# Running sums of a state-space scan as rows from memory, and joined small products, beside streamed weight products

## The chip, the cores and the metric

One core of one Trainium2 chip runs the whole program. The metric is the time of one execution in microseconds (us), the median of the runs shown; lower is better. The engines are TensorE (PE), VectorE (DVE), ScalarE (ACT), GpSimd (POOL) and SyncE (SP), which here issues nearly all DMA transfers.

## What is computed

A backbone of two layers over 256 context tokens and 256 latent tokens of width 1024. Each layer modulates and normalises its tokens, feeds them to three mixers in parallel (a scan in both directions, a windowed attention, a convolution module), merges these by gates, and then has a feed-forward part (dense in layer 0, two of eight experts in layer 1). Layer 1 mixes the context only as far as the latents need it. The change lies in the scan and in attention:

```
def ssd_scan(xs, dt, a, bm, cm, h0):
    cs = jnp.cumsum(dt.reshape(nb, nc, q, n_groups, hg) * a.reshape(n_groups, hg), axis=2)
    cs_t = jnp.moveaxis(cs, 2, -1)
    decay = jnp.exp(jnp.where(lower, cs_t[..., :, None] - cs_t[..., None, :], -jnp.inf))
    scores = jnp.einsum('bclgn,bcsgn->bcgls', cm, bm)
    y_diag = jnp.einsum('bcgls,bcgels,bcsgep->bclgep', scores, decay, xd)
    decay_end = jnp.exp(cs[:, :, -1:] - cs)
    states = jnp.einsum('bcsgn,bcsge,bcsgep->bcgepn', bm, decay_end, xd)
    ...
    y_off = jnp.einsum('bclgn,bcgepn,bclge->bclgep', cm, h_in, jnp.exp(cs))
    y = (y_diag + y_off).reshape(nb, seq_len, n_heads, hp)

def na_context(q, k, v):
    s = jnp.einsum('bihd,bjhd->bhij', q, k, preferred_element_type=jnp.float32) * NA_HEAD_DIM ** -0.5
    p = jax.nn.softmax(s, axis=-1).astype(v.dtype)
    o = jnp.einsum('bhij,bjhd->bihd', p, v)
```

The scan has 16 heads of 64 in 2 groups, chunks of 128 tokens (four in layer 0's two streams, two of them latent) and two directions. Attention has 8 heads of 64.

## The kernel before

**Weight products.** Every product with a weight is three fp32r products (high by high, high by low, low by high halves; L204 to L206 in `wstat`, L250 to L252 in `wmov`). A weight tile of 128x1024 comes by one DMA on SP into one of three raw buffers (`raw`, L120); ACT makes its high half (L115), DVE its low half (L116). Tiles on PE are 128x512 with 512 tokens moving in layer 0, 256 in layer 1.

**Background.** `mix(l)` (L560) walks a list of steps, for layer 0 `glu dt qkv xbc ssd g1 p1 g2 p2 z g0 p0`. The weight products of these steps are the foreground. Beside them run generators: `conformer` (a convolution of 31 taps on DVE, L558, then a layer norm whose sums are the products `lnm`, L797), `attention` (L702) and `ssd` (L907). Each `yield` gives a price; `pump` lets a generator go on at a rate per weight product (`RATE`: conv 2.0, att 3.6, ssd 3.8 in layer 0). What a generator would do on PE it puts off: `defer(q, f, depth)` runs the function two steps later, so that its operands are ready when its place in PE's order comes, and `issue_after` the last weight product places it there. Attention must be done before `p1` (products named wb0na_out in layer 0), the conformer before `p2` (wb0conf_out), the scan before `p0` (wb0ssd_out); `g0` to `g2` are the gates (wg). A scheduler fixes each engine's order from these priorities before the run. Small products share four PSUM banks (`pw`); weight products have four more.

**Attention** (L702 to L776). For each pair of heads, a step makes the scores (S, L735), the exponentials, and then per head and query block puts off one `turned`: the transposes of the probabilities (L725) and the copy out of PSUM (L727, DVE for one head and ACT for the other). `values` puts off the products with v (po, L771), 64 columns wide.

**Scan.** `dt_path` (L839) makes the running sums `cs`. `states` (L917) puts off, per direction, one state product (st, L932). `ssd_y` (L994) makes, for each chunk, group, direction and four heads: four transposes that spread the running sum of a head over the partitions (cb, L1023), four differences with a floor on ACT (L1026), an exponential (L1027), the product with the scores (L1028), and puts off `diag`: four products (yd, L1035), each with 64 stationary columns. `off` puts off, per direction, four transposes (pe, L1050) of the exponentials, which ACT spread (rep, L1044), with four products (yo, L1051), a copy by ACT (E, L1054) and the sums on DVE.

Of the kernel before, what the change touches and what calls it, by code (L numbers as in the profile page):

```python
# [9 lines left out]
F32 = mybir.dt.float32  # L10
F32R = mybir.dt.float32r
I32 = mybir.dt.int32
AF = mybir.ActivationFunctionType
# [12 lines left out]
G = 2  # L26
# [27 lines left out]
class Body:  # L54
    def __init__(self, ctx, tc, a, out, dbg=None, stop=None):
        self.ctx, self.tc, self.a, self.out = ctx, tc, a, out
        self.dbg, self.stop = dbg, stop
        self.nc = tc.nc
        self.bg = []
        self.last = None  # L60
        ep = ctx.enter_context
        self.cst = ep(tc.tile_pool(name="cst", bufs=1))

# [638 lines left out]
    def attention(self, l, q, kT, v, nt, o_):  # L702
# [4 lines left out]
        q_ = []  # L707
        for q0, nk, lat in streams:
            nkb = nk // 128
            for hp in range(4):  # L710
# [5 lines left out]
                def turn(P, j, qb, PT=PT, nm=nm, nk=nk, nkb=nkb, st=st):  # L716

                    nc.vector.tensor_scalar(P, P, st[:, j, qb, 5:6], None, op0=ALU.mult)

                    def turned():  # L720
                        if not PT:
                            PT.update({i: self.t4(f"PT{nm}{i}").rearrange("p (k t) -> p k t", t=256) for i in range(2)})
                        pt = self.pw(f"PT{nm}{j}{qb}")
                        for kb in range(nkb):
                            nc.tensor.transpose(pt[:, kb * 128:(kb + 1) * 128], P[:, kb * 128:(kb + 1) * 128], self.con("id"))  # L725
                        ev = nc.scalar.copy if j else nc.vector.tensor_copy
                        ev(PT[j][:, :nkb, qb * 128:(qb + 1) * 128], pt[:, :nk].rearrange("p (k t) -> p k t", t=128))  # L727
                    self.defer(q_, turned)
                if lat:
                    for qb in range(2):  # L730
# [17 lines left out]
                        for j in range(2):  # L748
                            turn(P[j], j, qb)
                            yield 1.7  # L750
                else:
# [6 lines left out]
                    for j in range(2):  # L758
# [5 lines left out]
                        for qb in range(2):  # L764
                            turn(P[j][:, qb * 256:(qb + 1) * 256], j, qb)
                        yield 1.5
# [7 lines left out]
                self.defer(q_, values)  # L774
                yield 0.5
        yield from self.undefer(q_)  # L776

# [121 lines left out]

    def xs_t(self, b, half, name):  # L900
# [6 lines left out]
    def ssd(self, l, nt):  # L907
# [9 lines left out]
        def states(b, dirs, use):  # L917
# [6 lines left out]
            for g in range(G):  # L924
                px = self.xs_t(b, g, "s" + nm)
                for r in dirs:
# [67 lines left out]
    def ssd_y(self, nm, b, hin, q_):  # L994
# [5 lines left out]
        ecs = self.wk.tile([128, 2, H], F32, name=f"ecs{nm}{b}", tag="ecs", bufs=2)  # L1000
        nc.scalar.activation(ecs, cs[:, b], AF.Exp)
# [9 lines left out]
        for g in range(G):  # L1011
# [5 lines left out]
            st = {}  # L1017
            for r in range(2):
                for hq in range(2):
                    h0 = g * 8 + hq * 4  # L1020
                    pb = self.pw(f"cb{nm}{b}{g}{r}{hq}")
                    for i in range(4):
                        nc.tensor.transpose(pb[:, i * 128:(i + 1) * 128], cs[:, b, r, h0 + i:h0 + i + 1].to_broadcast([128, 128]), self.con("id"))  # L1023
                    M = self.t2(f"M{nm}{b}{g}{r}{hq}").rearrange("p (h l) -> p h l", h=4)
                    for i in range(4):
                        nc.scalar.activation(M[:, i, :], pb[:, i * 128:(i + 1) * 128], AF.Relu, bias=cs[:, b, r, h0 + i:h0 + i + 1], scale=-1.0)  # L1026
                    nc.scalar.activation(M, M, AF.Exp, scale=-1.0)  # L1027
                    nc.vector.tensor_tensor(M, M, scm[:, r, g, None, :].to_broadcast([128, 4, 128]), op=ALU.mult)  # L1028

                    def diag(r=r, hq=hq, M=M, g=g, xd=xd, st=st):  # L1030
                        if "pd" not in st:
                            st["pd"] = self.pw(f"yd{nm}{b}{g}")
                        for i in range(4):
                            hl = hq * 4 + i
                            nc.tensor.matmul(st["pd"][64 * (i % 2):64 * (i % 2) + 64, (hl // 2) * 128:(hl // 2 + 1) * 128],  # L1035
                                             xd[r][:, hl * 64:(hl + 1) * 64], M[:, i, :],
                                             start=(r == 0 and hl < 2), stop=(r == 1 and hl > 5), skip_group_check=True)
                    self.defer(q_, diag)
                    yield 1.8
            for r in range(2):  # L1040
                if hin[r] is None:
                    continue
                rep = self.t2(f"rep{nm}{b}{g}{r}")
                nc.scalar.activation(hd(rep), ecs[:, r, g * 8:(g + 1) * 8, None].to_broadcast([128, 8, 64]), AF.Copy)  # L1044

                def off(r=r, g=g, rep=rep, st=st):
                    pe = self.pw(f"pe{nm}{b}{g}{r}")
                    po = self.pw(f"yo{nm}{b}{g}{r}")
                    for i in range(4):
                        nc.tensor.transpose(pe[:, i * 128:(i + 1) * 128], rep[:, i * 128:(i + 1) * 128], self.con("id"))  # L1050
                        nc.tensor.matmul(po[:, i * 128:(i + 1) * 128], hin[r][:, g * 512 + i * 128:g * 512 + (i + 1) * 128],  # L1051
                                         u[10 + g][:, bs], start=True, stop=True)
                    E = self.t2(f"E{nm}{b}{g}{r}")
                    nc.scalar.activation(E, pe, AF.Copy)  # L1054
                    nc.vector.tensor_tensor(E, E, po, op=ALU.mult)
                    if "prev" in st:
                        nc.vector.tensor_tensor(E, E, st["prev"], op=ALU.add)
                    st["prev"] = E
                self.defer(q_, off)
                yield 1.2  # L1060

            def fin(g=g, st=st):
                prev = st["prev"]
                nc.vector.tensor_tensor(prev, prev, st["pd"], op=ALU.add)
                for i in range(4):
                    y = u[g * 4 + i][:, bs]
                    nc.vector.scalar_tensor_tensor(y, y, self.col("dsk", g * 4 + i), prev[:, i * 128:(i + 1) * 128], op0=ALU.mult, op1=ALU.add)
            self.defer(q_, fin)
            yield 1.2
# [556 lines left out]
    def run(self):  # L1626
# [3 lines left out]
        with ExitStack() as st:  # L1630
            self.pools(st, "a", 14, 2, 13, 3, 2, 4, hm=2, ev=3, mod=3)
# [141 lines left out]
```

## Time and profile before

| | |
|---|---|
| median of 3 runs | 2379.14 us (2379.12 to 2384.46) |
| profiled execution | 2381.03 us, span 2379.2 us |
| mean granted clock of PE | 0.983 |
| busy: PE, DVE, ACT | 2272.4, 1507.5, 1032.6 us |
| bytes moved | 469 MB, 197 GB/s over the span |

The span is what the profiler saw from the first to the last instruction; the 1.8 us beside it lie outside. Layer 0's mixer takes about the first 560 us of it; layer 1's ends at about 1412, and the experts take the rest. A busy time is the sum of records, which overlap on PE; how long an instruction takes there is read from the starts of two neighbours.

### The profile page before, as it was taken

What the parts mean: (1) busy time and instruction counts of PE and PEld (TensorE: products, weight loads), DVE (VectorE), ACT (ScalarE), POOL (GpSimd) and SP (SyncE); (2) the same over time, 40 slices, a digit from 0 to 9 for tenths busy, and PEclk for the clock granted to TensorE, in tenths of its full rate; (3) what the DMA queues carried; (4) which work ended last, traced back from release to release, by engine and by line L of the source; (5) the groups of instructions that cost most, each with busy time, mean ns of one, the idle gap of its engine ahead of it and who ended that gap; (6) DMA issues with size and microseconds to landing.
All of it is one profiled execution on the core that took longest, in us unless ns stands there. A gap on an engine that the chain in (4) does not pass through costs nothing.

```text
span 2379.2 us, 30278 instructions
## 1 busy us (share of the span) xinstructions
PE 2272.4 (96%) x11409; PEld 1667.2 (70%) x11409; DVE 1507.5 (63%) x2379; ACT 1032.6 (43%) x1690; POOL 18.2 (1%) x32
## 2 busy tenths in 40 slices
PE   7999999999999999999999999899999989999997
PEld 3776677677777777788877789775665656656554
DVE  3667999777667665537898765733432545555556
ACT  4335664643243222225447664433332345454454
POOL 0000000000000000000000000000000000000000
PEclk9999999999999999999999999989999999999998
DMA  7222232235435566333323234378888899999895
GB/s 280 82 89 71 80 124 71 67 121 163 142 98 173 180 192 193 118 98 100 125 93 102 72 102 150 112 298 321 335 326 322 339 365 368 355 391 347 339 364 224
DMA packets 106283, 469.33 MB, mean 197 GB/s; under 512 B 11536, under 2 KB 12048, under 8 KB 72336
## 3 DMA queue, kind: packets, MB, share of 16 engines
q1 hardware_dynamic: 105280, 464.69, 54.3%
q10 hardware_dynamic: 848, 2.62, 0.3%
q8 instruction: 91, 1.49, 0.3%
q14 instruction: 64, 0.52, 0.1%
HBM read 466.22 MB, written 1.05 MB: 196 GB/s over the span
## 4 chain that ended last, share of the span: by engine, by line
PE 75%; issue 10%; DVE 7%; DMA 4%; ACT 4%; POOL 0%; SPq 0%; POOLq 0%; DVEq 0%; ACTq 0%
PE er L1524 8%; PE nn L1406 7%; PE e L1524 4%; PE edr L1524 4%; PE ndn L1431 4%; DMA adaw<-in_ada_w_dram 3%; PE ed L1524 2%; PE wg L204 2%; PE wg L206 2%; PE wg L205 2%; DVE adac L372 1%; DVE ccv L558 1%; PE fd L251 1%; PE fd L252 1%; PE fd L250 1%
## 5 line engine op out<-in xcount | busy, mean ns | idle before, releaser
L372 DVE SCALAR_TENSOR_TENSOR adac<-adaw,sc,adac 128x512 f32<-128x512 f32 x224 | 159.8, 747 | 55.5 <-DMA adaw<-in_ada_w_dram 54.6
L116 DVE TENSOR_TENSOR l_er<-r_er,h_er 128x1024 fp32r<-128x1024 f32 x132 | 154.6, 1219 | 58.6 <-ACT h_er L115 57.5
L1406 PE MATMUL nn<-r_ngun,xn 128*64 128x512 f32 (+1 forms) x768 | 169.3, 561 | 0.0
L115 ACT ACTIVATE h_er<-r_er 128x1024 fp32r<-128x1024 f32 x132 | 133.3, 1053 | 40.5 <-DMA r_er<-in_moe_gu_dram 28.0
L204 PE MATMUL wg<-hHm,h_wg 128*128 128x512 f32 (+1 forms) x384 | 136.2, 356 | 0.9 <-ACT h_wg L115 0.9
L205 PE MATMUL wg<-hLm,h_wg 128*128 128x512 f32 (+1 forms) x384 | 130.7, 341 | 0.0
L206 PE MATMUL wg<-hHm,l_wg 128*128 128x512 f32 (+1 forms) x384 | 128.9, 341 | 0.6 <-DVE l_wg L116 0.6
L1524 PE MATMUL er<-h_er,gHp 128*128 128x512 f32 (+1 forms) x288 | 110.7, 390 | 17.7 <-ACT h_er L115 17.7
L1406 PEld LDWEIGHTS nn<-r_ngun,xn 128*64 128x64 f32 x768 | 54.4, 137 | 92.1 <-issue 85.1
L1524 PE MATMUL er<-h_er,gLp 128*128 128x512 f32 (+1 forms) x288 | 108.1, 381 | 0.0
L116 DVE TENSOR_TENSOR l_e<-r_e,h_e 128x1024 fp32r<-128x1024 f32 x44 | 52.1, 1222 | 63.2 <-ACT h_e L115 61.5
L1431 PE MATMUL ndn<-r_ndn,hnn 128*64 128x512 f32 x352 | 87.4, 598 | 0.0
L558 DVE SCALAR_TENSOR_TENSOR ccv<-cu,cols,ccv 128x488 f32<-128x488 f32 (+14 forms) x120 | 84.8, 730 | 1.0
L1411 ACT ACTIVATE ntn<-nn 128x512 f32<-128x512 f32 (+1 forms) x24 | 13.5, 561 | 163.5 <-PE nn L1406 163.5
L1421 DVE TENSOR_TENSOR hnn<-npn,nsn 128x256 f32<-128x256 f32 (+1 forms) x24 | 9.6, 401 | 117.5 <-ACT nsn L1419 117.5
L1524 PE MATMUL er<-l_er,gHp 128*128 128x512 f32 (+1 forms) x288 | 84.0, 380 | 0.0
L1524 PEld LDWEIGHTS er<-h_er,gHp 128*128 128x128 f32 x288 | 55.2, 192 | 40.2 <-ACT h_er L115 28.0
L115 ACT ACTIVATE h_wg<-r_wg 128x1024 fp32r<-128x1024 f32 x48 | 50.8, 1060 | 74.1 <-PE wg L205 47.7
L204 PEld LDWEIGHTS wg<-hHm,h_wg 128*128 128x128 f32 x384 | 72.7, 189 | 13.8 <-issue 5.0
L116 DVE TENSOR_TENSOR l_edr<-r_edr,h_edr 128x1024 fp32r<-128x1024 f32 x66 | 77.5, 1220 | 6.0 <-ACT h_edr L115 4.5
L206 PEld LDWEIGHTS wg<-hHm,l_wg 128*128 128x128 f32 x384 | 72.2, 190 | 10.0 <-DVE l_wg L116 2.0
L205 PEld LDWEIGHTS wg<-hLm,h_wg 128*128 128x128 f32 x384 | 72.8, 190 | 7.4 <-issue 1.4
(657 smaller groups left out, 6071.8 us busy)
## 6 DMA issues: line engine op xcount, KB each, us to landing
r_ngun<-in_moe_gu_dram SPq DMA_DIRECT2D x88, 1024.0 KB, 6.7
r_er<-in_moe_gu_dram SPq DMA_DIRECT2D x66, 1024.0 KB, 7.2
r_ndn<-in_moe_down_dram SPq DMA_DIRECT2D x44, 1024.0 KB, 7.8
adaw<-in_ada_w_dram SPq DMA_DIRECT2D x160, 256.0 KB, 3.1
r_edr<-in_moe_down_dram SPq DMA_DIRECT2D x33, 1024.0 KB, 7.0
r_wg<-in_w_in_dram SPq DMA_DIRECT2D x48, 512.0 KB, 3.5
r_e<-in_moe_gu_dram SPq DMA_DIRECT2D x22, 1024.0 KB, 7.9
r_xbcL<-in_w_in_dram SPq DMA_DIRECT2D x24, 512.0 KB, 3.5
```

Source lines behind the costliest of these rows:

```text
L115: nc.scalar.activation(Hd, src, AF.Copy)
L116: nc.vector.tensor_tensor(Ld, src, Hd.bitcast(F32), op=ALU.subtract)
L204: mm(out, wh, xh, start=(first and kk == 0), stop=False, skip_group_check=True)
L205: mm(out, wh, xl, start=False, stop=False, skip_group_check=True)
L206: self.last = mm(out, wl, xh, start=False, stop=(kk == kc - 1), skip_group_check=True).ins
L250: mm(out, xh, w[0][:, k, :], start=(kk == 0), stop=False, skip_group_check=True)
L251: mm(out, xh, w[1][:, k, :], start=False, stop=False, skip_group_check=True)
L372: nc.vector.scalar_tensor_tensor(d, w, c, d, op0=ALU.mult, op1=ALU.add)
L558: nc.vector.scalar_tensor_tensor(y[:, :, a:b], x[:, :, a + s:b + s], w[:, k:k + 1], y[:, :, a:b], op0=ALU.mult, op1=ALU.add)
L1406: mm(ps[64 * h:64 * h + 64, :n], x[kk], w[:, h, k, :], start=(kk == 0), stop=(kk == KD - 1), skip_group_check=True)
L1431: mm(ps[64 * h:64 * h + 64], hT[:, kk * 64:(kk + 1) * 64], w[:, h, k, :], start=(kk == 0), stop=(kk == fc - 1), skip_group_check=True)
L1524: mm(ps[s][j], st[kk], w[p][:, k, :], start=(kk == 0 and p == 0 and q == 0), stop=(kk == kc - 1 and p == 1), skip_group_check=True)
```

## The change

- `dt_path` turns the running sums of all chunks once (two transposes) and writes them to memory as rows (`csd`). `ssd_y` loads eight heads' rows spread over 128 partitions (`cb`, 512 KB, three buffers) where it had transposed them, and loads the rows for the exponentials into E (two loads of 128 KB for each direction), on which ACT then takes the exponential in place. The transposes L1023 and L1050, the spreading copies L1044 and the copies L1054 go.
- `diag` holds eight heads of a direction, and the second one also the products yo of both directions and the sums after them.
- `states` puts off both directions' state products as one function.
- In attention both heads of a pair are turned in one function (for the context both query blocks, too), and the value products stand ahead of the next turn's transposes.
- All of these are put off by one step instead of two; the pool of 128x512 scratch tiles has 9 buffers instead of 13.

(The lines that go from `ssd_y`, `diag`, `off` and `fin` among them, are in the listing above and left out at the end.)

```diff
+        self.dram = ep(tc.tile_pool(name="dram", bufs=1, space=bass.MemoryType.DRAM))
...
-                def turn(P, j, qb, PT=PT, nm=nm, nk=nk, nkb=nkb, st=st):
-
-                    nc.vector.tensor_scalar(P, P, st[:, j, qb, 5:6], None, op0=ALU.mult)
+                def turn(P, qbs, PT=PT, nm=nm, nk=nk, nkb=nkb, st=st):
+
+                    for j in range(2):
+                        for qb in qbs:
+                            nc.vector.tensor_scalar(P[j][qb], P[j][qb], st[:, j, qb, 5:6], None, op0=ALU.mult)
 
                     def turned():
                         if not PT:
                             PT.update({i: self.t4(f"PT{nm}{i}").rearrange("p (k t) -> p k t", t=256) for i in range(2)})
-                        pt = self.pw(f"PT{nm}{j}{qb}")
-                        for kb in range(nkb):
-                            nc.tensor.transpose(pt[:, kb * 128:(kb + 1) * 128], P[:, kb * 128:(kb + 1) * 128], self.con("id"))
-                        ev = nc.scalar.copy if j else nc.vector.tensor_copy
-                        ev(PT[j][:, :nkb, qb * 128:(qb + 1) * 128], pt[:, :nk].rearrange("p (k t) -> p k t", t=128))
-                    self.defer(q_, turned)
+                        pts = [self.pw(f"PT{nm}{j}{qbs[0]}") for j in range(2)]
+                        n = len(qbs) * 128
+                        for f in joined:
+                            f()
+                        joined.clear()
+                        for j in range(2):
+                            for kb in range(nkb):
+                                for i, qb in enumerate(qbs):
+                                    c = kb * n + i * 128
+                                    nc.tensor.transpose(pts[j][:, c:c + 128], P[j][qb][:, kb * 128:(kb + 1) * 128], self.con("id"))
+                        for j in range(2):
+                            ev = nc.scalar.copy if j else nc.vector.tensor_copy
+                            ev(PT[j][:, :nkb, qbs[0] * 128:qbs[0] * 128 + n], pts[j][:, :nkb * n].rearrange("p (k t) -> p k t", t=n))
+                    self.defer(q_, turned, 1)
...
-                            turn(P[j], j, qb)
-                            yield 1.7
+                        turn([{qb: p} for p in P], (qb,))
+                        yield 3.4
...
-                        for qb in range(2):
-                            turn(P[j][:, qb * 256:(qb + 1) * 256], j, qb)
-                        yield 1.5
+                        yield 1.2
+                    turn([{qb: p[:, qb * 256:(qb + 1) * 256] for qb in range(2)} for p in P], (0, 1))
+                    yield 0.6
...
-                self.defer(q_, values)
-                yield 0.5
+
+                self.defer(q_, lambda f=values: joined.append(f), 1)
         yield from self.undefer(q_)
+        yield 1.0
+        with self.behind():
+            for f in joined:
+                f()
...
+        pr = self.pw("csr" + nm)
+        nc.tensor.transpose(pr[:, :128], fl(cs), self.con("id"))
+        row = self.t2("csr" + nm)[:, :128]
+        nc.vector.tensor_copy(row, pr[:, :128])
+        self.csd = self.dram.tile([128, 128], F32, name="csd" + nm, tag="csd" + nm)
+        nc.sync.dma_start(self.csd, row)
...
-                    xe = self.t2(f"xe{nm}{b}{r}{g}")
-                    nc.vector.tensor_tensor(hd(xe), hd(px), hb(we, b, r, g), op=ALU.mult)
-
-                    def state(r=r, g=g, xe=xe):
-                        ps = self.pw(f"st{nm}{b}{r}{g}")
-                        nc.tensor.matmul(ps, Bp[:, g * 128:(g + 1) * 128], xe, start=True, stop=True)
-                        use(r, g, ps)
-                    self.defer(q_, state)
-                    yield 1.8
+                    xe[r] = self.t2(f"xe{nm}{b}{r}{g}")
+                    nc.vector.tensor_tensor(hd(xe[r]), hd(px), hb(we, b, r, g), op=ALU.mult)
+
+                def state(g=g, xe=xe):
+                    ps = {r: self.pw(f"st{nm}{b}{r}{g}") for r in dirs}
+                    for r in dirs:
+                        nc.tensor.matmul(ps[r], Bp[:, g * 128:(g + 1) * 128], xe[r], start=True, stop=True)
+                    for r in dirs:
+                        use(r, g, ps[r])
+                self.defer(q_, state, 1)
+                yield 1.8 * len(dirs)
...
-        ecs = self.wk.tile([128, 2, H], F32, name=f"ecs{nm}{b}", tag="ecs", bufs=2)
-        nc.scalar.activation(ecs, cs[:, b], AF.Exp)
+        rows = lambda r, g: self.csd[b * 32 + r * 16 + g * 8:b * 32 + r * 16 + (g + 1) * 8, :]
+        cb = {}
+
+        def load(r, g):
+
+            if (r, g) not in cb and g < G:
+                cb[r, g] = self.p4.tile([128, 8, 128], F32, name=f"cb{nm}{b}{r}{g}", tag="cb", bufs=3)
+                nc.sync.dma_start(cb[r, g], rows(r, g)[None].to_broadcast([128, 8, 128]))
+        load(0, 0)
...
-            st = {}
+            st, M = {}, {}
             for r in range(2):
+                load(*((1, g) if r == 0 else (0, g + 1)))
+                pb = cb[r, g]
                 for hq in range(2):
                     h0 = g * 8 + hq * 4
-                    pb = self.pw(f"cb{nm}{b}{g}{r}{hq}")
+                    m = M[r, hq] = self.t2(f"M{nm}{b}{g}{r}{hq}").rearrange("p (h l) -> p h l", h=4)
                     for i in range(4):
-                        nc.tensor.transpose(pb[:, i * 128:(i + 1) * 128], cs[:, b, r, h0 + i:h0 + i + 1].to_broadcast([128, 128]), self.con("id"))
-                    M = self.t2(f"M{nm}{b}{g}{r}{hq}").rearrange("p (h l) -> p h l", h=4)
+                        nc.scalar.activation(m[:, i, :], pb[:, hq * 4 + i, :], AF.Relu, bias=cs[:, b, r, h0 + i:h0 + i + 1], scale=-1.0)
+                    nc.scalar.activation(m, m, AF.Exp, scale=-1.0)
+                    nc.vector.tensor_tensor(m, m, scm[:, r, g, None, :].to_broadcast([128, 4, 128]), op=ALU.mult)
+                    if hq == 0:
+                        yield 1.8
+
+                E = {}
+                for d in range(2) if r else ():
+                    if hin[d] is None:
+                        continue
+                    E[d] = self.t2(f"E{nm}{b}{g}{d}").rearrange("p (i l) -> p i l", i=4)
+                    for j in range(2):
+                        nc.sync.dma_start(E[d][64 * j:64 * j + 64], rows(d, g).rearrange("(i j) l -> j i l", j=2)[j][None].to_broadcast([64, 4, 128]))
+
+                def diag(r=r, M=M, g=g, xd=xd, st=st, E=E):
+                    if r == 0:
+                        st["pd"] = self.pw(f"yd{nm}{b}{g}")
+                    E = {d: e.rearrange("p i l -> p (i l)") for d, e in E.items()}
+                    for e in E.values():
+                        nc.scalar.activation(e, e, AF.Exp)
+                    for hl in range(8):
+                        nc.tensor.matmul(st["pd"][64 * (hl % 2):64 * (hl % 2) + 64, (hl // 2) * 128:(hl // 2 + 1) * 128],
+                                         xd[r][:, hl * 64:(hl + 1) * 64], M[r, hl // 4][:, hl % 4, :],
+                                         start=(r == 0 and hl < 2), stop=(r == 1 and hl > 5), skip_group_check=True)
+                    po = {d: self.pw(f"yo{nm}{b}{g}{d}") for d in E}
+                    for d in E:
+                        for i in range(4):
+                            nc.tensor.matmul(po[d][:, i * 128:(i + 1) * 128], hin[d][:, g * 512 + i * 128:g * 512 + (i + 1) * 128],
+                                             u[10 + g][:, bs], start=True, stop=True)
+                    if r == 0:
+                        return
+                    prev = st["pd"]
+                    for d, e in E.items():
+                        nc.vector.tensor_tensor(e, e, po[d], op=ALU.mult)
+                        nc.vector.tensor_tensor(e, e, prev, op=ALU.add)
+                        prev = e
                     for i in range(4):
...
+                        y = u[g * 4 + i][:, bs]
+                        nc.vector.scalar_tensor_tensor(y, y, self.col("dsk", g * 4 + i), prev[:, i * 128:(i + 1) * 128], op0=ALU.mult, op1=ALU.add)
+                self.defer(q_, diag, 1)
+                yield 1.8 if r == 0 else 4.2
...
-            self.pools(st, "a", 14, 2, 13, 3, 2, 4, hm=2, ev=3, mod=3)
+            self.pools(st, "a", 14, 2, 9, 3, 2, 4, hm=2, ev=3, mod=3)
```

In PE's order, where the gate products wg of layer 0 run (yd is L1035's product, xty turns the scan's inputs, numbers tell buffers apart), there stands before:

```order
L205 MATMUL wg_2_2427<-hLm_256,h_wg_0_2431 128x512
L206 MATMUL wg_2_2427<-hHm_254,l_wg_0_2432 128x512
L1035 MATMUL ydS_2485<-MS_2414,xdS_2405 64x128 x4
L1023 MATMUL cbS_2510<-con_t,cs_669 128x128 x4
L904 MATMUL xtyS_2576<-con_t,uL_4_1131 128x128 x2
L904 MATMUL xtyS_2576<-con_t,uL_6_1132 128x128 x2
L204 MATMUL wg_3_2428<-hHm_254,h_wg_0_2431 128x512
L205 MATMUL wg_3_2428<-hLm_256,h_wg_0_2431 128x512
L206 MATMUL wg_3_2428<-hHm_254,l_wg_0_2432 128x512
L204 MATMUL wg_3_2428<-hHm_254,h_wg_0_2431 128x512
L1023 MATMUL cbS_2585<-con_t,cs_669 128x128 x4
L205 MATMUL wg_3_2428<-hLm_256,h_wg_0_2431 128x512
```

and now, in two places of that stretch:

```order
L206 MATMUL wg_0_2410<-hLm_258,h_wg_1_2475 128x512
L207 MATMUL wg_0_2410<-hHm_256,l_wg_1_2476 128x512
L1077 MATMUL ydS_2496<-MS_2403,xdS_2397 64x128 x4
L1077 MATMUL ydS_2496<-MS_2434,xdS_2397 64x128 x4
L925 MATMUL xtyS_2545<-con_t,uL_4_1139 128x128 x2
L925 MATMUL xtyS_2545<-con_t,uL_6_1140 128x128 x2
L205 MATMUL wg_1_2411<-hHm_256,h_wg_1_2475 128x512
L206 MATMUL wg_1_2411<-hLm_258,h_wg_1_2475 128x512
```

```order
L207 MATMUL wg_3_2413<-hHm_257,l_wg_2_2529 128x512
L1077 MATMUL ydS_2496<-MS_2459,xdS_2399 64x128 x4
L1077 MATMUL ydS_2496<-MS_2486,xdS_2399 64x128 x4
L1083 MATMUL yoS_2593<-uL_10_1142,hsS0c_2188 128x128 x4
L205 MATMUL wg_0_2410<-hHm_257,h_wg_3_2606 128x512
```

The transposes cb are gone, two runs of four yd products stand side by side, and yo follows the second pair at once, without transposes between.

In SP's order, about the first loads of na_out in layer 0 (adaw are modulation weights, cb and E the rows of running sums), there stands before:

```order
L120 DMA r_wb0na_out_0_2716<-in_na_out_dram 128x1024
L366 DMA adaw_3298<-in_ada_w_dram 128x512
L366 DMA adaw_3367<-in_ada_w_dram 128x512
L366 DMA adaw_3417<-in_ada_w_dram 128x512
L120 DMA r_wb0na_out_1_2801<-in_na_out_dram 128x1024
L366 DMA adaw_3454<-in_ada_w_dram 128x512
L366 DMA adaw_3496<-in_ada_w_dram 128x512
L120 DMA r_wb0na_out_0_2877<-in_na_out_dram 128x1024
L366 DMA adaw_3522<-in_ada_w_dram 128x512
L366 DMA adaw_3563<-in_ada_w_dram 128x512
```

and now:

```order
L121 DMA r_wb0na_out_0_2672<-in_na_out_dram 128x1024
L367 DMA adaw_3065<-in_ada_w_dram 128x512
L367 DMA adaw_3128<-in_ada_w_dram 128x512
L1031 DMA cbS_2554<-csd_698 128x1024
L1068 DMA ES_2493<-csd_698 64x4x128 x2
L121 DMA r_wb0na_out_1_2731<-in_na_out_dram 128x1024
L1031 DMA cbS_2705<-csd_698 128x1024
L367 DMA adaw_3155<-in_ada_w_dram 128x512
L367 DMA adaw_3206<-in_ada_w_dram 128x512
L1031 DMA cbS_2722<-csd_698 128x1024
L121 DMA r_wb0na_out_0_2809<-in_na_out_dram 128x1024
```

Loads of rows now stand between the loads of weights, so that a weight load can be the next in the queue behind one of them.

## Rows read from the trace of the kernel before

**Rows 1.** The page: span, busy time of the engines, shares of the chain that ended last

```profile
span 2379.2 us, 30278 instructions
...
PE 2272.4 (96%) x11409; PEld 1667.2 (70%) x11409; DVE 1507.5 (63%) x2379; ACT 1032.6 (43%) x1690; POOL 18.2 (1%) x32
...
PE 75%; issue 10%; DVE 7%; DMA 4%; ACT 4%; POOL 0%; SPq 0%; POOLq 0%; DVEq 0%; ACTq 0%
```

**Rows 2.** Windows: stretch, length, busy us and (x) of each engine, PEclk, DMA share, GB/s

```profile
200.00:300.00 100.00, 99.79 (x454) 67.90 (x454) 92.73 (x198) 59.11 (x123) 0.00 (x0) 1.00 0.24 77
300.00:411.00 111.00, 111.00 (x611) 84.55 (x609) 104.76 (x162) 62.81 (x127) 0.00 (x0) 1.00 0.33 102
411.00:462.00 51.00, 46.29 (x272) 34.39 (x271) 34.24 (x59) 34.63 (x69) 1.11 (x1) 0.95 0.14 48
1300.00:1412.00 112.00, 107.34 (x822) 90.98 (x821) 78.24 (x126) 77.09 (x155) 0.00 (x0) 0.98 0.27 86
```

**Rows 3.** Timeline of PE, 315 to 328: start us, length us, line, operation, shapes, count

```profile
316.13 0.60 PE L1023 MATMUL cbS<-con_t,cs 128*128 128x128 f32 x4
316.48 0.47 PE L204 MATMUL wg<-hHm,h_wg 128*128 128x512 f32 x1
316.80 0.39 PE L205 MATMUL wg<-hLm,h_wg 128*128 128x512 f32 x1
...
325.93 0.39 PE L205 MATMUL wg<-hLm,h_wg 128*128 128x512 f32 x1
326.16 0.39 PE L206 MATMUL wg<-hHm,l_wg 128*128 128x512 f32 x1
326.48 0.66 PE L1035 MATMUL ydS<-MS,xdS 128*64 128x128 f32 x8
327.06 0.50 PE L204 MATMUL wg<-hHm,h_wg 128*128 128x512 f32 x1
327.40 0.40 PE L205 MATMUL wg<-hLm,h_wg 128*128 128x512 f32 x1
327.64 0.40 PE L206 MATMUL wg<-hHm,l_wg 128*128 128x512 f32 x1
```

**Rows 4.** Timeline of PE, 255 to 257

```profile
255.54 1.12 PE L735 MATMUL S<-kTL,qL 64*128 64x512 f32 x2
256.59 0.50 PE L205 MATMUL xbcL<-hLm,h_xbcL 128*128 128x512 f32 x1
256.93 0.40 PE L206 MATMUL xbcL<-hHm,l_xbcL 128*128 128x512 f32 x1
```

**Rows 5.** Groups on PE: out<-in, shapes, xcount, busy us, mean ns, idle before

```profile
L1035 PE MATMUL ydS<-MS,xdS 128*64 128x128 f32 x384 | 36.6, 290 | 0.4 <-DVE MS L1028 0.4
L1023 PE MATMUL cbS<-con_t,cs 128*128 128x128 f32 x192 | 31.7, 281 | 0.1
L1050 PE MATMUL peS<-con_t,repS 128*128 128x128 f32 x80 | 19.7, 285 | 1.3 <-DVE ES L1055 1.3
```

**Rows 6.** Groups on ACT

```profile
L667 ACT ACT_TABLE_LOAD x13 | 16.7, 1283 | 0.2
L1044 ACT ACTIVATE repS<-ecsS 128x512 f32<-128x512 f32 x20 | 12.7, 643 | 0.0
L1054 ACT ACTIVATE ES<-peS 128x512 f32<-128x512 f32 x20 | 12.0, 598 | 23.1 <-PE peS L1050 22.9
```

**Rows 7.** Chain of waits, 395 to 470; then one wait of PE, us, times, longest

```profile
410.42 0.73 DVE ccv L558
411.19 1.98 PE lnm L797 x4
...
PE wb0conf_out L204 <- ACT g L667: 4.8, 1, 4.8
```

**Rows 8.** Waits of SP's queue, 100 to 560; then a DMA issue, KB, us to landing

```profile
SPq L120 <- DVE l_wg L116: 105.3, 16, 20.3
...
r_wg<-in_w_in_dram SPq DMA_DIRECT2D x48, 512.0 KB, 3.5
```

More of the change, by code (lines that the diff above doesn't have):

```diff
@@ L706, in attention @@
         streams = ([(0, 256, False)] if l == 0 else []) + [(nt - 256, 512, True)]
-        q_ = []
+        q_, joined = [], []
         for q0, nk, lat in streams:
@@ L747, in attention @@
                         nc.vector.reciprocal(s[:, :, 5], s[:, :, 5])
-                        for j in range(2):
-                            turn(P[j], j, qb)
-                            yield 1.7
+                        turn([{qb: p} for p in P], (qb,))
+                        yield 3.4
                 else:
@@ L925, in states @@
                 px = self.xs_t(b, g, "s" + nm)
+                xe = {}
                 for r in dirs:
-                    xe = self.t2(f"xe{nm}{b}{r}{g}")
-                    nc.vector.tensor_tensor(hd(xe), hd(px), hb(we, b, r, g), op=ALU.mult)
-                    def state(r=r, g=g, xe=xe):
-                        ps = self.pw(f"st{nm}{b}{r}{g}")
-                        nc.tensor.matmul(ps, Bp[:, g * 128:(g + 1) * 128], xe, start=True, stop=True)
-                        use(r, g, ps)
-                    self.defer(q_, state)
-                    yield 1.8
+                    xe[r] = self.t2(f"xe{nm}{b}{r}{g}")
[8 more added lines that the diff above has]
+                yield 1.8 * len(dirs)
         def step(dst, prev, b, r, g, ps):
@@ L1022, in ssd_y @@
                     for i in range(4):
-                        nc.tensor.transpose(pb[:, i * 128:(i + 1) * 128], cs[:, b, r, h0 + i:h0 + i + 1].to_broadcast([128, 128]), self.con("id"))
-                    M = self.t2(f"M{nm}{b}{g}{r}{hq}").rearrange("p (h l) -> p h l", h=4)
-                    for i in range(4):
-                        nc.scalar.activation(M[:, i, :], pb[:, i * 128:(i + 1) * 128], AF.Relu, bias=cs[:, b, r, h0 + i:h0 + i + 1], scale=-1.0)
-                    nc.scalar.activation(M, M, AF.Exp, scale=-1.0)
@@ L1028, in ssd_y @@
[L1028 to L1069, printed above, removed]
+                        nc.scalar.activation(m[:, i, :], pb[:, hq * 4 + i, :], AF.Relu, bias=cs[:, b, r, h0 + i:h0 + i + 1], scale=-1.0)
```

## The prediction

> **What bounds the kernel now.** I read the page first. TensorE (PE) is busy for 96% of the span, and the chain of waits runs through PE for 75%, through DVE for 7%, through ACT for 4% [rows 1]. That is an average, so I read the stages in which the changed code runs by their windows [rows 2]: the mixer of layer 0 (about 100 to 560 us) and of layer 1 (about 1200 to 1412 us). Between 300 and 411 us PE is busy all 111.00 us, and DVE 104.76 of them: PE bounds, but DVE is close behind. Between 411 and 462 us PE is down to 46.29 of 51, DVE and ACT have 34 each. In layer 1 (1300 to 1412) PE has 107.34 of 112, ACT 77.09, DVE 78.24. So a product or transpose taken from PE is worth its time on PE, until DVE, 6 us behind in the tightest stretch, becomes what is waited for.
>
> The second reading is PE row by row [rows 3, 4], because a busy PE does not show what an instruction really takes: records overlap, and only the step from one start to the next is time. In a run of 128x512 fp32r weight products a step is 0.23 us (325.93 to 326.16). Four transposes of running sums take 0.35 us up to the next product (316.13 to 316.48), that product 0.32: 0.44 us, so about 0.11 us each. A run of eight records of L1035 (four half-width fp32 products, two records each) costs more than its own length: the product ahead of it takes 0.32 instead of 0.23 (+0.09), the run 0.58 (326.48 to 327.06), and the first product after it 0.34 instead of 0.23 (+0.11). For the products themselves I take the transposes' 0.109 us, since they too have 128 columns: 0.44 for four, so 0.15 of the 0.58 is no work either. The second product after the run still takes 0.24. One visit to this kind of product so has a fixed price of 0.09 + 0.15 + 0.11 + 0.01, by starts that are not rounded **0.37 us**, however many products it holds. A visit to the score products (L735, 64 rows deep) shows 0.34 on the way back (256.59 to 256.93), 0.11 too much, and I take the same 0.09 on the way in: 0.2 us.
>
> **The change, part by part.** The work on PE:
> - The 192 transposes that spread running sums (L1023) and the 80 that spread their exponentials (L1050) go [rows 5]; two transposes come (the rows written to memory). 270 x 0.109 = 29.4 us.
> - L1035 now does eight heads in one visit: over the program, in the new order, 62 visits become 30. 32 x 0.37 = 11.8 us. The products stay, 192 of them, 384 records [rows 5].
> - Value products join the next turn: 18 visits become 15, 3 x 0.37 = 1.1 us. Score products fall from 30 visits to 19: 11 x 0.2 = 2.2 us.
> - All small runs inside weight products go from 223 to 157; 46 of these 66 are counted above, the other 20 are transposes, at 0.02 to 0.1 us each: some 1.5 us.
>
> That is 46 us. As a second working I gave each PE product in both orders the step that its kind has in the trace behind the same kind of neighbour: 1440 us before and 1389 after up to the end of layer 1's mixer and routing, 52 us less, of it 35.5 in layer 0 and 16.4 in layer 1. I take **50 us** of work saved, with 29 (no visit saved at all) and 52 as its ends.
>
> What lies beside PE:
> - ACT loses 20 spreading copies (0.643 us each) and 20 copies out of PSUM (0.598), and gains 20 exponentials of the same 128x512 size, for which I take 0.643 [rows 6]; it gains 19 table loads in the new order, 55 to 74, at 1.283 us. 24.4 + 12.9 - 12.9 - 12.0, or 12 us more on ACT. With 63% of ACT busy from 300 to 411 and 69% in layer 1's stretch [rows 2] this is hidden, except at one place: the first product of wb0conf already waits 4.8 us for ACT [rows 7].
>
>   The Trainium skill ("ScalarE: Activation LUTs", section "Table sets: the hidden batching unit") says that functions should be batched by table set, since each switch of set is a load of about 2.7 us; by that figure the 19 loads would be an estimated 51 us of ACT. The trace has 1283 ns for each, and the sum above goes by that. The rule speaks against this change, which mixes exponentials into more places; what it would do here is rival 3.
> - DVE keeps its work: the evictions of turned weights are half as many and twice as long.
> - SP gets 24 loads of 512 KB (a row of sums spread over 128 partitions), 40 of 128 KB, two writes. For the first kind the nearest row is a 512 KB weight load, 3.5 us from issue to landing [rows 8]. SP mostly waits for buffers: 105.3 us in 16 waits for the halves of wg alone. About 18 MB more, some 400 us in which the scan runs, are 45 GB/s on top of the 77 to 102 of those stretches, which are 24% to 33% of the DMA engines' time [rows 2]: under half in all. I cost them at nothing; the cover is SP's waiting time, and if it is gone, rival 5 has the price. The 128 KB loads, in 512-byte pieces, have no row of their kind; between nothing and 3.5 us each, and issued a whole deferred step ahead of their use, I take nothing.
> - The merged steps hold several small PSUM banks at once (one for L1035's sums, two for the state products; two turned blocks). Before, the same step held three as well. I take nothing; rival 4 is the other end.
>
> **Where it stalls next.** The conformer's convolution is on DVE, and its last tap ends at 411.15; the layer-norm products on PE follow at once [rows 7]. From 200 us up to there DVE was idle for 7.3 + 6.2 = 13.5 us. PE has 9 us less ahead of these products in the new order (they also stand later in it). DVE can follow by what of its idle time waited for PE: between 0 and 9 us come back as a wait, I take 5. From there to the first wb0conf product PE has 27 us of work in the new order, where it had 43; DVE and ACT have 34 in that stretch [rows 2], so 6 to 12 us come back, I take 6. In layer 1 PE keeps about 91 of work beside 78 on DVE: 0 to 5, I take 1. **Given back: 12 us.**
>
> 50 - 12 = 38. The profiled execution took 2381.0 us (its span 2379.2); 2381 - 38 = 2343, and since the median of the three runs is 1.9 us below that execution, I say **2341 us**. A change under 0.3%, 7.1 us, could hardly be told from none.
>
> **The rivals.**
> 1. Nothing is given back: DVE was late only because PE was. For it: DVE's 13.5 idle us ahead of 411 are more than the 9 that are asked for. Against it: 104.76 of 111 in the last stretch. 2381 - 50 - 2 = 2329 us.
> 2. DVE's convolution and the layer-norm chain give back 25 us (9 and 12 at the two places, 4 in layer 1), or only the transposes count as saved. 2381 - 25 - 2 = 2354 us. For it: DVE's 6 idle us from 300 to 411.
> 3. Table loads come to be waited for: a load stands ahead of the halves and gates that ACT makes for PE. All 24 us on top of the 12 given back: 2341 + 24 = 2365 us. For it: wb0conf's wait; against it: ACT idle for 37% of the stretch.
> 4. The change does not do what it says: the joined steps wait in PE's order for small PSUM banks, and each of some 30 double steps loses about as much (1.6 us, a state product pair's time and an eviction) as the transposes had cost. About 2379 us, no change.
> 5. **Slower**: SP issues in order, and a load of sums waits for one of three buffers that ACT frees, with the weight loads queued behind it. If it is 3.5 us, a landing time, on the path for each of 24 loads: 84 us, 2379 - 50 + 84 = 2413 us. It decides from 50 / 24 = 2.1 us a load. For it: weight loads follow right behind such loads in the new order of SP. Against it: SP issues weights as soon as a buffer is free, so a small delay is covered by the other raw buffers, and ACT is not late.
>
> **How the numbers follow.** Chances: forecast 0.50 (2334 to 2349), rival 1 0.18, rival 2 0.16, rival 3 0.05, rival 4 0.05, rival 5 0.06. Faster by over 0.3% is the first four, 0.89, less a little for the tails: 0.88; within 0.3% 0.06; slower 0.06. The range takes in rivals 1 to 3 and the ends of the saved work: 2324 (52 saved and nothing given back, 2327, and 3 for the scatter of the runs) to 2366.
>
> **What would show it.** Right: no L1023 or L1050 transposes, L1035's successor in 30 visits, PE's busy time down by about 50 us with ACT's up by 12; the layer-norm products start about 4 to 9 us earlier than 411, and the first wb0conf product waits longer than before for ACT or DVE; the FFN and the experts keep their length. Wrong: PE waiting in the mixers for weight halves behind loads on SP, a busy DVE with PE idle before 411 us, or a saving of PE time well beside 50 us.

## The result, and the profile after

| | before | after |
|---|---|---|
| median of 6 runs each | 2380.98 us | 2362.55 us (2361.89 to 2364.11) |
| ratio | | 0.9917 (0.9905 to 0.9929) |
| profiled execution, span | 2381.0, 2379.2 | 2362.4, 2360.6 |

18.4 us faster, where 38 were forecast. The page after, against [rows 1]:

```profile
span 2360.6 us, 29841 instructions
...
PE 2226.2 (94%) x11139; PEld 1638.1 (69%) x11139; DVE 1506.7 (64%) x2377; ACT 1052.5 (45%) x1679; POOL 18.5 (1%) x32
...
PE 74%; issue 10%; DVE 7%; ACT 4%; DMA 4%; POOL 0%; SPq 0%; POOLq 0%; DVEq 0%; ACTq 0%
```

PE's busy time fell by 46.2 us, and the span by 18.6: PE now idles 27.6 us more. So the work went, and came back as waits. To place them I priced each PE product of each kernel's order as in the prediction's second working and took that sum from the time between the same two products in the trace; what is left are waits (and low clock). These are estimates: their level hangs on the prices, so only differences between kernels are used, and these are no surer than 3 us. All up to the routing of layer 1, in us:

| kernel | PE's work | waits to the last layer-norm product, layer 0 | from there to the next stage's first product | to layer 1 | layer 1 |
|---|---|---|---|---|---|
| before | 1440.5 | 18.5 | 6.7 | 26.5 | 18.7 |
| after | 1388.6 | 18.6 | **24.0** | 25.5 | **34.7** |

51.9 less work, 32 more waits: 17 in one stretch of layer 0 and 16 in layer 1, less 1 between the two. The stretch of layer 0 by windows (columns as in [rows 2]), and PE's waits in layer 0's mixer (us, times, longest):

```profile
404.00:430.00 26.00, 23.23 (x135) 18.02 (x134) 18.41 (x33) 12.79 (x28) 1.02 (x1) 0.97 0.16 57
430.00:456.00 26.00, 12.20 (x68) 6.62 (x67) 19.55 (x35) 25.78 (x47) 0.00 (x0) 0.70 0.62 164
```

```profile
PE wb0conf_out L205 <- ACT g L668: 10.7, 1, 10.7
PE ydS L1077 <- DVE MS L1058: 4.9, 3, 2.2
```

ACT is busy for 25.78 of the 26 us from 430 to 456, and PE for 12.20. Some of what ACT does there, from its timeline (g is a gate, made out of the sums wg):

```profile
430.12 1.28 ACT L829 ACT_TABLE_LOAD   x1
431.41 0.82 ACT L829 ACTIVATE ccv<-ccv,cols 128x512 f32<-128x512 f32 x1
432.25 1.28 ACT L1057 ACT_TABLE_LOAD   x1
433.54 0.63 ACT L1057 ACTIVATE MS<-MS 128x512 f32<-128x512 f32 x1
434.08 1.55 ACT L1056 ACTIVATE MS<-cbS,cs 128x128 f32<-128x128 f32 x5
...
453.37 1.28 ACT L668 ACT_TABLE_LOAD   x1
454.66 1.09 ACT L668 ACTIVATE g<-wg 128x512 f32<-128x512 f32 x2
```

and PE beside it:

```profile
424.59 0.39 PE L207 MATMUL wg<-hHm,l_wg 128*128 128x512 f32 x1
427.22 0.66 PE L1077 MATMUL ydS<-MS,xdS 128*64 128x128 f32 x8 [2.24 <-DVE MS L1058]
...
434.95 1.03 PE L1077 MATMUL ydS<-MS,xdS 128*64 128x128 f32 x8 [1.74 <-DVE MS L1058]
...
455.31 0.79 PE L205 MATMUL wb0conf_out<-c,h_wb0conf_out 128*128 128x512 f32 x1 [10.75 <-ACT g L668]
455.90 0.63 PE L206 MATMUL wb0conf_out<-cL,h_wb0conf_out 128*128 128x512 f32 x1
456.33 0.63 PE L207 MATMUL wb0conf_out<-c,l_wb0conf_out 128*128 128x512 f32 x1
```

The last gate product runs at 424.59 (456.96 before), and its sums lie in a PSUM bank until ACT evicts them at 454.66, because ACT, in order, first makes the scan's factors MS and, between them, the normalised pieces ccv, with a table load at each turn: eight loads in the stretch, 10.3 us, where the kernel before has five. The four banks for weight products are full of such sums: four evictions of g are still to come, at 454.66 and 461.52. In layer 1 the waits are in two places:

```profile
1289.67 0.63 PE L735 MATMUL PT<-con_t,P 128*128 128x128 f32 x4 [1.69 <-DVE P L721]
1291.59 0.87 PE L735 MATMUL PT<-con_t,P 128*128 128x128 f32 x4 [1.30 <-DVE st L753]
1295.51 1.94 PE L735 MATMUL PT<-con_t,P 128*128 128x128 f32 x8 [3.05 <-DVE P L721]
```

```profile
PE ydS L1077 <- DVE MS L1058: 4.8, 2, 3.8
PE PT L735 <- DVE P L721: 4.7, 2, 3.0
PE PT L735 <- ACT P L754: 2.5, 2, 2.0
PE PT L735 <- DVE st L753: 1.3, 1, 1.3
```

The prices themselves held: a joined visit (one run of small products) behind a gate product takes, by the starts, 0.32 for the product ahead and 1.02 for sixteen records (two times 0.44 and 0.14), where each visit of [rows 3] took 0.32 and 0.58 for eight:

```profile
324.31 0.39 PE L207 MATMUL wg<-hHm,l_wg 128*128 128x512 f32 x1
324.63 1.09 PE L1077 MATMUL ydS<-MS,xdS 128*64 128x128 f32 x16
325.65 1.16 PE L1083 MATMUL yoS<-uL,hsS0c 128*128 128x128 f32 x8
```

### The profile page after: what moved, and what is told of

It is laid out like the page before. It is cut to its first block, busy times and chain, and to the rows that moved or that the text cites. A ratio compares the mean times of both kernels' runs of the same rounds, so it can differ in the third digit from the quotient of the medians.

```text
span 2360.6 us, 29841 instructions
## 1 busy us (share of the span) xinstructions
PE 2226.2 (94%) x11139; PEld 1638.1 (69%) x11139; DVE 1506.7 (64%) x2377; ACT 1052.5 (45%) x1679; POOL 18.5 (1%) x32
## 4 chain that ended last, share of the span: by engine, by line
PE 74%; issue 10%; DVE 7%; ACT 4%; DMA 4%; POOL 0%; SPq 0%; POOLq 0%; DVEq 0%; ACTq 0%
PE er L1551 8%; PE nn L1433 7%; PE e L1551 4%; PE edr L1551 4%; PE ndn L1458 4%; DMA adaw<-in_ada_w_dram 3%; PE ed L1551 2%; DVE adac L373 2%; PE wg L205 2%; PE wg L207 1%; PE wg L206 1%; PE fd L252 1%; PE fd L253 1%; PE fd L251 1%; PE xbcL L205 1%
## 5 line engine op out<-in xcount | busy, mean ns | idle before, releaser
L373 DVE SCALAR_TENSOR_TENSOR adac<-adaw,sc,adac 128x512 f32<-128x512 f32 x224 | 159.6, 747 | 52.0 <-DMA adaw<-in_ada_w_dram 51.1
L559 DVE SCALAR_TENSOR_TENSOR ccv<-cu,cols,ccv 128x496 f32<-128x496 f32 (+14 forms) x120 | 85.0, 729 | 1.1
```

The lines of the kernel that those rows point to most:

```text
L373: nc.vector.scalar_tensor_tensor(d, w, c, d, op0=ALU.mult, op1=ALU.add)
L559: nc.vector.scalar_tensor_tensor(y[:, :, a:b], x[:, :, a + s:b + s], w[:, k:k + 1], y[:, :, a:b], op0=ALU.mult, op1=ALU.add)
```

## Experiments

Theory A: ACT's order holds PE up where PE's work got shorter. B: functions put off by one step reach PE before their operands. C: the loads of rows delay the weights behind them. Each group of runs has runs of the kernel before beside it, to which its ratios are taken; their medians are 2383.0 to 2384.0 us, and 2381.0 beside the changed kernel, so times of different groups can be off by 3 us against each other. A scheduler fixes the orders of all engines from the priorities, so an edit meant for ACT's order moves PE's order too.

**z products ahead of p2** (after, layer 0: `g2 p2 z g0 p0` becomes `g2 z p2 g0 p0`).

> The changed kernel with one edit: in layer 0 the z products stand ahead of p2 (the order that layer 1 has already), so that PE has weight products while the layer norm's chain runs on DVE and ACT. Theory A (the 17 us that layer 0 gave back were lost because the weight products ran out before the chain over ACT was through): 2362.5 - 12 to 17, or 2345 to 2351, and the first wb0conf product waits for nothing. Theory B (the joined functions are put off by only one step, so PE reaches them before their operands are there): the wait of 10.7 us moves but the waits of yd and of the turns stay, 2350 to 2358. Theory C (loads of rows ahead of weights on SP): no change, 2360 to 2364.

2367.5 us, ratio to before 0.9927 (0.9911 to 0.9944): none of the three. The wait moved, whole, to the first z product:

```profile
PE zL L205 <- ACT g L668: 10.9, 1, 10.9
```

A z product needs none of the normalised pieces, and it waits as long. So PE did not lack work here: the next weight product needs a bank, and the banks wait for ACT's evictions of the gate. That sharpened theory A.

**Pieces and evictions first on ACT** (after).

```diff
-    PR = dict(w=10000, ev=5000, conv=0, att=5000, ssd=5000, ada=5000, norm=20000, init=30000, lg=-20000)
+    PR = dict(w=10000, ev=9000, conv=0, att=5000, ssd=5000, ada=5000, norm=20000, init=30000, lg=-20000)
...
-            nc.scalar.activation(cv[i], cv[i], AF.Silu, bias=self.col("lb", i), scale=self.col("lg", i))
+            with self.tc.high_priority(offset=9000):
...
+                nc.scalar.activation(cv[i], cv[i], AF.Silu, bias=self.col("lb", i), scale=self.col("lg", i))
```

> The changed kernel with one edit of priorities: the four normalised pieces of the convolution (silu and split) and the evictions of the weight products come ahead of the scan's work on ACT, where they stood behind it. The table loads fall from 74 to 62 by it. Theory A: the first wb0conf product no longer waits 10.7 us for ACT, and 10 to 20 us come back: 2343 to 2353. Theory B: the scan's waits get longer, since ACT makes its factors later: 2358 to 2368. Theory C: 2360 to 2364.

2345.7 us (0.9838, 0.9821 to 0.9854), 17 us faster than the changed kernel (19 by the ratios), as theory A expected. The same windows as above: PE is busy nearly throughout, at full clock.

```profile
404.00:430.00 26.00, 25.44 (x141) 20.52 (x141) 17.46 (x31) 14.24 (x25) 1.02 (x1) 1.00 0.14 46
430.00:456.00 26.00, 26.00 (x155) 20.23 (x154) 16.06 (x22) 24.77 (x48) 0.00 (x0) 1.00 0.50 154
```

The waits in the stretch fall from 24.0 to 1.0, in layer 1 from 34.7 to 26.9; ahead of the layer norm they rise from 18.6 to 27.2; the evictions now also pass attention's work there, and PE waits 5.7 us for probabilities P in layer 0, where the changed kernel has no such wait. Two things besides ACT's order moved: PE's last gate product now runs at 435.10 instead of 424.59, and four table loads lie between the layer norm and wb0conf instead of eight.

**Two steps** (after; `defer(..., 1)` becomes 2 in all joined functions).

> The changed kernel with the joined functions put off by two steps again, as in the kernel before, instead of one (the pool of scratch tiles stays at 9). Theory A: within 4 us of 2362.5, since the chain over ACT is as long as before. Theory B: PE's waits for the factors of yd (4.9 us in layer 0, 4.8 in layer 1) and for the probabilities (8.5 us in layer 1) go, and with them 10 to 18 us: 2345 to 2352. Theory C: 2360 to 2364.

2362.1 us, the same as after: theory B falls as the main cause. Layer 0's stretch stays at 23.3; layer 1 gets 4 us better, and other places worse.

**The rows alone** (before, with `csd`, `cb` and E loaded; nothing joined).

> The kernel before with the running sums from memory as rows and nothing else (yd in runs of four heads, yo per direction, two steps; the pool of scratch tiles has 9 buffers, as space asks). By the steps of PE's new order PE has 38 us less work. Theory A: the chain over ACT in the layer norm's stretch gives back 10 to 15 of them: 2355 to 2362 beside 2381 of the kernel before, and the joins are then worth little on the clock. Theory B: put off by two steps, nearly all 38 show: 2343 to 2350. Theory C: the loads cost as they do in the changed kernel, 2355 to 2365 with waits for weight halves.

2378.7 us (0.9978, 0.9968 to 0.9988): 38 us of work gone by the steps and 5 us won. Waits: 22.5 in the stretch, 39.0 in layer 1. All expectations were too fast; the same wait for a gate's eviction is there without any join:

```profile
PE wb0conf_out L205 <- ACT g L668: 11.5, 1, 11.5
```

**Halves of the edit, and the edit elsewhere.**

> The changed kernel with one half of the priority edit: only the evictions of weight products (the gates' sigmoids among them) come ahead of the scan's work on ACT; the normalised pieces stay behind it. Theory A1 (the four accumulation banks are held by gates that ACT has not evicted, so any next weight product must wait): most of the 17 us of both edits, 2346 to 2352. Theory A2 (the normalised pieces themselves are what wb0conf waits for): 2358 to 2364.

> The changed kernel with the other half: only the four normalised pieces come ahead of the scan's work on ACT; the evictions stay where they were. Theory A1: 2357 to 2364, the first wb0conf product still waits for a gate's eviction. Theory A2: 2346 to 2352.

> The kernel before with both priority edits and nothing else. Theory A (ACT's order there matters because the change shortened PE's way to it): the kernel before waits 4.8 us at this place and 1 to 3 by the low clock around it, so 2373 to 2380 beside 2381. Rival D (the edits are worth 17 us by themselves, and tell nothing of the change): 2362 to 2368.

> The kernel before with the rows from memory, and both priority edits. By PE's steps it has 35 us less work than before. Theory A: with ACT's order mended most of it shows, 2350 to 2358, where the rows alone gave 2378.7. Theory B (the rest is lost since PE comes to small products before their operands): 2366 to 2376.

2358.7, 2356.9, 2395.8 and 2364.0 us; the first falls where A2 put it, the second just below A1's range, the other two where no theory had put them. Neither half does it alone: the stretch keeps 13.6 and 12.0 of 24.0. The halves don't tell the bank from the pieces. With evictions alone first, the gate's evictions still come only at 455.67, behind the same factors and pieces, and wb0conf waits 11.6 us for them; the higher priority did not bring them forward there. With the pieces alone first, the wait moved to the scan's factors:

```profile
PE ydS L1078 <- DVE MS L1059: 8.8, 1, 8.8
```

Evictions ahead of everything cost 9 us of waits before the layer norm in the changed kernel and 13 in the kernel before, which gets slower by them (1.0055, 1.0038 to 1.0072), against both of its expectations. Among kernels with both edits, the differences are near the work by the steps: 2395.8 to 2345.7 is 50 us, with 49; 2395.8 to 2364.0 is 32, with 35. But their base is the kernel before made 13 us slower. Against the kernel before as it is, both edits bring the changed kernel 38 us and the rows alone 19.

**The edit in its place.** The next four move, beside the pieces, only the third gate's evictions.

> The changed kernel with the priority edit cut down to its place: the normalised pieces and only the evictions of the third gate come ahead of the scan's work on ACT; all other evictions stay, since moving them too had cost 10 us of waits ahead of the layer norm. Theory A (ACT's order between the last gate product and wb0conf held 17 us back): the wait at wb0conf is gone without that loss, 2336 to 2344. Rival E (both evictions and pieces only helped since all evictions moved): 2352 to 2360.

> The kernel before with the same cut-down edit. Theory A: it can win no more than its own waits in that stretch, 6.7 us by the steps: 2372 to 2381. Rival D (the edit is worth the same in both kernels): 2362 to 2368.

> The changed kernel with the cut-down edit and with the attention of the kernel before. By PE's steps it has 8.4 us more work. If the joined turns lose nothing: 8 us slower than the same kernel with the joins, 2345 to 2352. If the joins put PE's transposes in front of probabilities that are not there yet (the waits of 6 us and more around 1290 us in layer 1), they take back what they save: no difference, within 3 us.

> The changed kernel with the cut-down edit and all joined functions put off by two steps. With layer 0's stretch mended, theory B for layer 1 (one step is too short for the probabilities and the factors): the waits of layer 1, 32 us by the steps beside 16 in the kernel before, fall by 8 to 14, so 8 to 14 us faster than the same kernel with one step. Theory A for layer 1 too (ACT's order, its table loads among it): within 4 us of it.

2354.4, 2377.7, 2358.6 and 2357.5 us. The first falls short of theory A and into the range of rival E: the stretch goes to 7.8, but 8 us come back behind it, 3.5 of them as z's wait for DVE's evictions of wb0conf. The wait at wb0conf itself did not go:

```profile
PE wb0conf_out L205 <- ACT g L670: 6.5, 1, 6.5
```

PE's last gate product stands at 425.57 here, and ACT takes most of the four pieces and a table load ahead of the gate's first eviction at 431.85. This speaks for part of what both edits won having come with PE's later gate products, and not with ACT's order at this place alone; no run parts the two. The kernel before wins the little it can, as theory A said. The joined attention is worth 4.2 us of its 8.4, and two steps are no better (3 us slower, within the spread that theory A allowed).

**Evictions first from where they matter.** `PR["ev"]` is 9000 from `g2` on in layer 0, from `ssd` on in layer 1, and 5000 elsewhere; pieces first. One kernel has the old attention, one loads E a step earlier:

```diff
-                E = {}
-                for d in range(2) if r else ():
+                E = {} if r == 0 else E0
+                for d in range(2) if r == 0 else ():
...
+                if r == 0:
+                    E0, E = E, {}
```

> The changed kernel with the normalised pieces first on ACT, and the evictions of weight products first from the third gate on in layer 0 and from the scan's start on in layer 1; ahead of that evictions stay, since there the edit of all evictions cost 10 us. If ACT's order is the cause in both layers: no waits at wb0conf, layer 1's waits fall by some 8 us, and nothing is lost ahead: 2330 to 2340. If the 10 us ahead only moved behind: 2344 to 2350.

> The same with the attention of the kernel before, 7.5 us more work on PE by the steps. If the joined turns wait for probabilities in layer 1: within 3 us of the joined one, with 5 to 7 us less wait between the v products and wb1na in layer 1. If not: 6 to 9 us slower.

> The same as the first with the loads of rows for E issued one step earlier, ahead of the first direction's factors instead of behind the second's. ACT then does not stand before an E that has not landed (14 us of waits in the changed kernel). If these waits hold up the factors queued behind and so PE: 4 to 10 us faster than the first. If ACT has time there: within 3 us.

> The kernel before with the same orders. Its own waits in the two places are 12 us in layer 0 and 16 in layer 1. If the orders matter because the change made PE faster there: 2366 to 2378, so that 35 to 45 us lie between the two kernels with the same orders, near the 49 of PE's steps. If they help both alike: 2350 to 2360.

2344.8, 2351.2, 2341.1 and 2382.0 us. The first is no faster than both edits everywhere (2345.7): it falls where its expectation has the waits ahead only move behind, and wb0conf still waits 6.5 us for a gate. The last is the same as before (0.9990, 0.9980 to 1.0000), slower than either of its cases; 37 us lie between the two kernels with these orders, within the 35 to 45 expected. **The kernel with E loaded early is the fastest of all**, 0.982 of before (0.9804 to 0.9837), and 21 us faster than the changed kernel. Early E is worth 3.7 us, between its two cases; all four runs are faster than all four without it. ACT's wait in mended_both, and ACT's group of these exponentials (mean ns, then idle before) in the kernel with early E:

```profile
ACT ES L1081 <- DMA ES<-csd: 17.5, 6, 4.5
```

```profile
L1084 ACT ACTIVATE ES<-ES 128x512 f32<-128x512 f32 x20 | 12.4, 621 | 1.1 <-DMA ES<-csd 1.0
```

In layer 1 the waits by the steps are 28.9 for mended_both (its profiled execution took 2350.9 us, 6 above its median, so its waits are the upper end), 23.5 with the old attention and 26.9 with early E, beside 34.7 after and 20.9 for the kernel before with the same orders. On the clock the joins of attention win 6.4 of their 7.5 us (2351.2 to 2344.8), the case in which they don't wait; so the 5 us more of waits that they show by the steps are at most partly theirs.

## Why the prediction was partly wrong

- **Saved work: right.** 50 us forecast; 51.9 by the steps of the order, 46.2 by PE's busy time. Between two kernels with the same orders, 50 and 37 us show as time. 38 of the 51.9 lie in the order with the rows alone; the price per visit was seen again, as quoted above.
- **Given back: wrong.** 12 us forecast (5, 6 and 1 at three places), 32 by the steps: 0, 17 and 16, less 1 in between. 51.9 less 32 is the gain, within 1 us of the span's 18.6. So two terms were too small, and the next two points are the steps that failed.
- **Layer 0, from the layer norm to wb0conf: the first step that failed.** "DVE and ACT have 34 in that stretch [rows 2], so 6 to 12 us come back, I take 6." The place and the wait for ACT were right, the size was not. I laid PE's 27 us beside a sum of busy time, as if that work could start with the stretch and run in any order. ACT's work starts only when the norm's chain and the scan release it, and ACT takes it in order: it is idle for half of 404 to 430, full from 430 to 456, and what PE needed stood last. The stretch is 51.1 us long, where it had been 49.6, with 16 us less work for PE: 17 came back.
- **Layer 1, "0 to 5, I take 1": the other step that failed.** 16 us. The 78 us of DVE's busy time were laid beside PE's 91 in the same way; the trace shows PE at the turns and at yd ahead of their operands, 4.7 us for P and 4.8 us for MS. About 6 of the 16 go with ACT's order, 2 with E's late loads and at most 5 with the joined turns (after to mended_both, early E, old attention). These shares are differences of estimates, the last one is not borne out by the clock, and 3 us or more have no cause shown.
- **Ahead of the layer norm: the range held, the 5 us taken did not.** The last layer-norm product starts 8.4 us earlier (404.22 for 412.59), as the 9 us of work ahead of it say; DVE took none of it back.
- **ACT's work: right in kind.** 55 table loads became 74. ACT is 19.9 us longer busy, where I had 12.
- **Rivals.** The time fell near rivals 2 and 3, both with ACT or DVE in PE's way; that it lies in the stated range is due to the room made for these. The price was that of one queue's order more than of all table loads: the stretch has three loads more than before, 3.8 us of the 17. The kernel with evictions first has 59 loads and 2358.7 us, the one with pieces and evictions first 62 and 2345.7. Still, the edits that helped in this stretch also took loads out of it (two to four are left of eight); with evictions alone first all eight stay, and so does more than half of the wait. No run parts the order from the loads. The Trainium skill ("ScalarE: Activation LUTs", section "Table sets: the hidden batching unit") would have functions batched by set; the trace agrees that alternating sets is dear at this place, at 1.283 us a load and not 2.7 (from the end of ccv at 432.23, with the load, to the next MS at 433.54 it is 1.31), but the count of loads did not order the times. Rival 5, theory C of the experiments, did not come: PE waits for weight halves 1 to 2 us in each mixer. Rival 4 did not come either: the waits of PE that look like one for a small PSUM bank are 1.6 and 0.3 us.

## What to carry to other kernels

Work taken off a full engine is worth its steps only up to the next place at which that engine needs something from an engine that works in order; look there not for that engine's busy share, but for what stands ahead of the needed instruction in its queue, and when that can begin. Once all accumulation banks hold finished sums, the eviction that frees one gates the next weight product, whichever it is, so a filler moved in behind it hides nothing (z waited 10.9 us where wb0conf had waited 10.7). What a change is worth depends on the queue orders beside it: the rows showed 5 us with the orders left alone and 19 with both edits, 32 if the kernel before is given the same edits, which cost it 13. With the best order found for each, at 0.982 and 0.998 of before, the two kernels lie some 38 of the 50 us of work apart, though more orders were tried for the changed kernel.

## What was unexpected of the hardware

The 512 KB loads that spread rows over partitions landed in 4.6 us and the 128 KB ones, a quarter of the bytes in 512-byte pieces, in 4.2 (weights: 3.6):

```profile
cbS<-csd SPq DMA_DIRECT2D x24, 512.0 KB, 4.6
ES<-csd SPq DMA_DIRECT2D x40, 128.0 KB, 4.2
```

And a wait of PE costs more than itself: in the window from 430 to 456 the granted clock is 0.70, from 452 to 456 it is 0.50, and after 10.75 us without work wb0conf's products start 0.43 us apart instead of 0.23, the 1.2 GHz level instead of 2.4. Seven such steps, from 455.90 to 458.89, cost some 1.4 us more than at the higher level.
